# Encoder trunk on one core: sums leave GpSimd, convolution products stand ahead of their inverses, residual written in pieces

## Chip, cores and metric

One core of a Trainium2 chip runs the whole program. The metric is the device time of one execution in microseconds; lower is better. A core has five engines with a queue of instructions each: TensorE (PE, matmuls), VectorE (DVE), ScalarE (ACT), GpSimd (POOL) and SyncE (SP, which here only issues transfers). Each engine takes its own queue strictly in order and waits where an instruction needs what another engine has not yet made.

## The reference

Two layers over two inputs of batch 1 with shared weights, a prompt of 512 tokens and a sample of 256, of 1024 features, in float32. Each layer is a SwiGLU, a mixer (windowed attention on half of the features, a two-sided long convolution on the other half) and a second SwiGLU. Each is followed by a layer norm of the scaled residual plus the result.

```python
def _trunk(x, c, ...):
    for l in range(DEPTH):
        mod = (jax.nn.silu(c) @ ada_w[l] + ada_b[l]).reshape(B, N_MOD, D_MODEL)
        h = _modulate(x, mod[:, 0], mod[:, 1])
        f = _swiglu(h, ffn1_wi[l], ffn1_wo[l])
        x = _layer_norm(ALPHA * x + 0.5 * (1.0 + mod[:, 2][:, None, :]) * f, ln_g[l, 0], ln_b[l, 0])
        h = _modulate(x, mod[:, 3], mod[:, 4])
        z = h @ w_in[l]
        q, k, v, hz = jnp.split(z, [...], axis=-1)
...
        o_attn = _window_attention(q, k, v, sink[l])
        hz = _short_conv(hz, hy_conv_w[l], hy_conv_b[l])
        x0, x1, hv = jnp.split(hz, 3, axis=-1)
        filt = _hyena_filters(...)
        o_hy = _bidir_long_conv(hv * x1, filt, hy_bias[l]) * x0
        o = jnp.concatenate([_rms_norm(o_attn, grp_norm_g[l, :D_ATTN]),
                             _rms_norm(o_hy, grp_norm_g[l, D_ATTN:])], axis=-1) @ w_out[l]
        x = _layer_norm(ALPHA * x + (1.0 + mod[:, 5][:, None, :]) * o, ln_g[l, 1], ln_b[l, 1])
        h = _modulate(x, mod[:, 6], mod[:, 7])
        f = _swiglu(h, ffn2_wi[l], ffn2_wo[l])
        x = _layer_norm(ALPHA * x + 0.5 * (1.0 + mod[:, 8][:, None, :]) * f, ln_g[l, 2], ln_b[l, 2])
    return x
```

The long convolution (`_bidir_long_conv`) is a product of spectra: transform, multiply by the filter's spectrum, transform back.

## The kernel before

**Layout.** Features lie on the 128 partitions and the 768 tokens side by side, so `x`, `h` and the like are 8 tiles `d` of 128 x 768; `SEQ[0]` is the prompt's 512 columns and `SEQ[1]` the sample's 256. A float32 product is made from halves: ScalarE rounds a tile to its high half (`acopy`), another engine writes the low half `lo = x - hi` (a `tt`, a sum or difference of two tiles, on the engine named by `eng`), and TensorE makes three matmuls of the halves. Weights come as units of 128x1024 through SyncE's queue into a raw tile (`slot_r`), are split into a `slot_w` tile by `w_ahead`, and are taken in a fixed order by `w_take`. FFN products use a fast scheme of seven products; `joined` and `mixed` prepare its sums of activations and `prep_*` those of weights. Buffers are a few numbered slots per kind (`slot_s` 10 large ones, `slot_w` 6, `slot_r` 7, `slot_t` 6 scratch, `bank` 8 in PSUM); a new tile takes the slot that is free longest, and its writer waits for the last reader of the old one.

**Order.** There is no scheduler: the order on each engine is the order in which the Python code calls the operations. All instructions carry line L70, the wrapper that issues them, so the profile is read by tile names.

**The prologue.** `first_h` makes the first modulated input from `x`, then the loop at the end of `_program` runs six units of FFN 1 of layer 0 (`part[0].unit(i)`) with one `pump(1)` each. `pump` advances the ada steps, by which the modulation of later parts is computed: a step loads a 128x1024 block `ada_t` and takes two weighted sums of it on VectorE (CUSTOM_DVE) into `mods`. The very first also needs `silu(c)` on ScalarE from `c_row`. The residual's home in HBM, `x_spill`, is filled by one copy of `x_in` on GpSimd's queue.

**The mixer.** `run` in `mixer` orders it: units 4 to 11 are projections (4 to 9 with their short convolutions in `hyena_in`, 10 and 11 for `x0`), q/k/v groups follow with `side(i)` called after the i-th, then the attention's steps `u`. The convolution works on two halves `Hyena(0)` and `Hyena(1)` of the channels: `u_spectrum` transforms, `products(a)` multiplies the spectrum for frequency tiles `a` = 0, 1, 2 and splits the result, `inverse(a)` transforms it back on TensorE, `gate(i)` adds it to the output. A product with `a` below 2 is 16 multiplications, sums and low halves of 128x512, of which GpSimd makes 5 today (a third product term, and one low half); pm sums, the low halves of weights, of the RMS-normed groups (`Rms.apply`) and the sums of squares of attention blocks (`block_squares`) are GpSimd's too (`w_state["eng"] = gp` while the mixer runs).

**Norms and the residual.** `final` ends a part: output tiles come for the sample first, then for the prompt; `norm.add` sums `x` and its square over the tiles into `S` and `Q`, `norm.stats` and `bcast` make mean and scale, `norm.apply` writes the new `x` (a scale on GpSimd into `slot_s`) and the next `h`, `norm.low` its low halves. `after()` then writes the two halves `x.t[0]` and `x.t[1]` of the residual to `x_spill`, 1.5 MB each, and the next part's buffers take their slots.

## Time and profile before

| | us |
|---|---|
| median of 3 runs | 2977.01 (2975.27 to 2978.75) |
| the profiled execution | 2977.46 |
| its span on the core | 2975.2 |
| TensorE busy | 2853.4 |
| VectorE busy | 2101.6 |
| ScalarE busy | 1368.4 |
| GpSimd busy | 576.0 |
| mean granted TensorE clock | 0.982 of full speed |

The span is the time from the first to the last instruction; 2.3 us of the execution lie around it. Busy time of an engine is the sum of its instructions, so a stall of TensorE is the difference, and a stretch in which TensorE is granted half its clock counts as busy though it does half the work. What an idle engine waited for (its releaser) is inferred from semaphores. Times inside the span count from its start.

### The profile page before, as it was taken

Reading aid. Unit: us, or ns where it says so; the run is one execution under the profiler, and the core shown is the slowest. Engines: PE = TensorE matmul, PEld = TensorE weight load, DVE = VectorE, ACT = ScalarE, POOL = GpSimd, SP = SyncE. Lnnn points to the kernel's source line nnn. Section 1 sums busy time; section 2 is a strip of 40 time slices with the busy share of each in tenths; the row PEclk is TensorE's granted clock in tenths of the full one; section 3 lists DMA queues with packets and bytes.
Section 4 is the critical chain, followed back from the end, with each engine's and each line's share of the span. In section 5 each row is a group of like instructions: output and inputs, shape, how many; then the busy total and the mean of one; then the engine's idle time right before and its main releaser. Section 6 shows DMA issues by size and latency. Waiting matters only on the chain. (4 is left out here: it accounts for less than half of the span.)

```text
span 2975.2 us, 42222 instructions
## 1 busy us (share of the span) xinstructions
PE 2853.4 (96%) x16468; PEld 2608.0 (88%) x16468; DVE 2101.6 (71%) x3604; ACT 1368.4 (46%) x2355; POOL 576.0 (19%) x602
## 2 busy tenths in 40 slices
PE   9969999999899999999999999999989999999998
PEld 3769999998897889999988999999879788999997
DVE  5587888876858777778477878546686887444557
ACT  3534444444258454444444444444425854444444
POOL 2400000024532400000031000003453240000002
PEclk9989999999999999999999999999999999999999
DMA  5536655633111126654422665353311112454342
GB/s 199 199 120 177 181 162 153 176 142 121 50 46 69 64 109 182 191 180 135 112 101 112 191 186 149 106 120 121 114 57 65 58 43 114 85 114 107 99 109 84
DMA packets 99375, 364.65 MB, mean 123 GB/s; under 512 B 13542, under 2 KB 16823, under 8 KB 94648
## 3 DMA queue, kind: packets, MB, share of 16 engines
q1 hardware_dynamic: 74968, 259.88, 24.4%
q0 software_dynamic: 24208, 102.08, 15.8%
q8 instruction: 129, 2.11, 0.3%
q14 instruction: 70, 0.57, 0.1%
HBM read 284.33 MB, written 80.74 MB: 123 GB/s over the span
## 5 line engine op out<-in xcount | busy, mean ns | idle before, releaser
L70 PE MATMUL bank<-slot_s,slot_w 128*128 128x384 f32 (+2 forms) x13176 | 2331.9, 337 | 60.9 <-ACT slot_t L70 19.4
L70 PEld LDWEIGHTS bank<-slot_s,slot_w 128*128 128x128 f32 x13176 | 2140.2, 191 | 229.5 <-DVE slot_w L70 24.7
L70 POOL DMA_DIRECT2D x_spill<-slot_t x128 | 110.7, 865 | 1450.0 <-ACT slot_t L70 1442.8
L70 DVE CUSTOM_DVE_ANT_0 slot_t<-slot_r,slot_r 128x1024 bf16<-128x1024 f32 x256 | 311.9, 1223 | 104.9 <-DMA x_spill<-slot_t 44.2
L70 DVE TENSOR_TENSOR slot_w<-slot_w,slot_w 128x1024 fp32r<-128x1024 f32 (+2 forms) x444 | 370.2, 865 | 4.1 <-ACT slot_w L70 1.6
L70 ACT ACTIVATE slot_w<-slot_w 128x1024 fp32r<-128x1024 f32 (+1 forms) x298 | 249.7, 839 | 113.6 <-DVE slot_w L70 113.6
L70 ACT ACTIVATE slot_t<-bank,tiny 128x512 f32<-128x512 f32 (+1 forms) x256 | 147.4, 580 | 305.4 <-PE bank L70 302.0
L70 ACT ACTIVATE slot_w<-slot_r 128x1024 fp32r<-128x1024 f32 (+1 forms) x194 | 189.0, 992 | 175.2 <-DVE slot_r L70 114.5
L70 DVE TENSOR_TENSOR slot_w<-slot_r,slot_w 128x1024 fp32r<-128x1024 f32 (+1 forms) x148 | 172.7, 1178 | 113.3 <-ACT slot_w L70 113.1
L70 ACT ACTIVATE slot_t<-slot_t 128x384 f32<-128x384 f32 (+2 forms) x161 | 84.0, 526 | 333.1 <-DVE slot_t L70 333.0
L70 DVE TENSOR_TENSOR slot_t<-bank,slot_t 128x384 f32<-128x384 f32 x228 | 125.4, 555 | 145.7 <-PE bank L70 73.4
L70 ACT ACTIVATE slot_s<-slot_t 128x768 fp32r<-128x768 f32 (+2 forms) x160 | 113.0, 715 | 169.6 <-DVE slot_t L70 169.3
L70 ACT ACTIVATE slot_t<-bank 128x384 f32<-128x384 f32 (+3 forms) x282 | 139.6, 496 | 105.3 <-PE bank L70 102.8
L70 DVE TENSOR_TENSOR slot_s<-slot_t,slot_s 128x768 fp32r<-128x768 f32 (+2 forms) x170 | 144.8, 854 | 47.5 <-ACT slot_s L70 38.9
L70 PE MATMUL bank<-slot_s,slot_r 128*128 128x384 f32 x912 | 172.2, 337 | 0.0
L70 PEld LDWEIGHTS bank<-slot_s,slot_r 128*128 128x128 f32 x912 | 160.8, 188 | 0.0
L70 POOL TENSOR_TENSOR slot_w<-slot_r,slot_w 128x1024 fp32r<-128x1024 f32 (+1 forms) x46 | 100.1, 2178 | 157.5 <-ACT slot_w L70 139.0
L70 DVE TENSOR_TENSOR slot_r<-slot_w,slot_r 128x512 fp32r<-128x512 f32 x76 | 52.0, 685 | 107.2 <-ACT slot_r L70 107.2
L70 ACT ACTIVATE slot_t<-slot_s 128x256 f32<-128x256 f32 (+1 forms) x132 | 65.7, 509 | 108.7 <-DVE slot_s L70 100.2
L70 POOL TENSOR_TENSOR slot_t<-slot_t,slot_s 128x256 f32<-128x256 f32 (+1 forms) x91 | 95.1, 1045 | 60.6 <-DVE slot_s L70 55.6
L70 PE MATMUL bank<-slot_w,slot_s 128*128 128x256 f32 x864 | 106.4, 283 | 0.0
L70 PEld LDWEIGHTS bank<-slot_w,slot_s 128*128 128x128 f32 x864 | 104.2, 190 | 0.0
(138 smaller groups left out, 2331.1 us busy)
## 6 DMA issues: line engine op xcount, KB each, us to landing
slot_r<-w_units SPq DMA_DIRECT2D x170, 512.0 KB, 4.7
slot_w<-w_units SPq DMA_DIRECT2D x146, 512.0 KB, 4.1
slot_r<-ada_t SPq DMA_DIRECT2D x128, 512.0 KB, 6.0
x_spill<-slot_t POOLq DMA_DIRECT2D x128, 384.0 KB, 5.3
slot_s<-x_spill POOLq DMA_DIRECT2D x12, 1536.0 KB, 7.1
x_spill<-slot_s POOLq DMA_DIRECT2D x10, 1536.0 KB, 7.0
slot_r<-ada_nat SPq DMA_DIRECT2D x16, 512.0 KB, 5.4
g_main<-slot_s POOLq DMA_DIRECT2D x4, 1536.0 KB, 10.1
```

Source lines behind the costliest of these rows:

```text
L70: return getattr(real, name)(*args, **kwargs)
```

## The change

Seven things are done at once.

- Low halves of weights in the mixers, of the RMS-normed groups, the pm sums, the sums of attention squares and all parts of the spectral products go from GpSimd to VectorE. GpSimd's queue falls from 572 to 390 rows as printed.
- The norm's sample sums `S` and all its sums of squares `Q` go to VectorE; the prompt's `S` stays on GpSimd.
- `run` puts each product two units ahead of its inverse; of the second half, inverses 1 and 2 with their gates go into `side(0)` and `side(1)`.
- `final` calls `spill(s, j)`: the sample thirds of the residual go out before the prompt's apply, the first prompt half after tile 3, the second after tile 7.
- `x_spill` is filled by four copies in the loop over the units instead of one ahead of it.
- `first_h` writes the first four tiles straight to `fast.full`, which saves `joined(0)` to `joined(3)`; the other `joined` and `mixed` stand in units 0 and 1.
- The ada steps start in unit 2: one each in units 2 and 3, two each in 4 and 5.

```diff
-            tt(w[:, 1], raw, f32(w[:, 0]), ALU.subtract, eng=w_state["eng"])
+            tt(w[:, 1], raw, f32(w[:, 0]), ALU.subtract)
...
-                tt(self.S[:, c], self.S[:, c], x, ALU.add, eng=gp)
+                tt(self.S[:, c], self.S[:, c], x, ALU.add, eng=vec if s else gp)
                 self.sq = (d, s, sq)
 
         def squares(self):
             if self.sq is not None:
                 d, s, sq = self.sq
                 q = self.Q[:, SEQ[s]]
-                tt(q, q, sq, ALU.add, eng=vec if s or d % 2 else gp)
+                tt(q, q, sq, ALU.add)
...
+        for j in range(2):
+            spill(1, j)
         norm.low()
         norm.low()
         norm.squares()
@@ -577,9 +579,10 @@
                 norm.bcast(0)
                 for d in range(ND):
                     norm.apply(0, d)
+                    if d % 4 == 3:
+                        spill(0, d // 4)
                 norm.low()
                 norm.low()
-                after()
...
     def first_h(d):
         for c, s in ((SEQ[0], 0), (SEQ[1], 1)):
             affine(h[0](d, c), x(d, c), G[:, d, s:s + 1], B[:, d, s:s + 1])
-            v = slot_t([SLEN[s]])
+            v = slot_t([SLEN[s]]) if d > 3 else part[0].fast.full(d, c)
             if s:
                 affine(v, x(d, c), G[:, d, s:s + 1], B[:, d, s:s + 1])
             else:
                 ts(v, x(d, c), G[:, d, s:s + 1], B[:, d, s:s + 1])
             tt(h[1](d, c), v, f32(h[0](d, c)), ALU.subtract, eng=vec if s else gp)
 
+    part = swiglu(x, *h, 0, 0)
...
-    gp.dma_start(x_spill, x_in)
...
-                        tt(pm[c][:, bk, j, :], u[:, :, :P], u[:, :, :P - 1:-1], op, eng=gp)
+                        tt(pm[c][:, bk, j, :], u[:, :, :P], u[:, :, :P - 1:-1], op)
...
-                n = len(terms[0])
-                if n > 2:
-                    rest = term(1, 2, eng=gp)
-                    plus(rest, 1, 3, term(1, 3, eng=gp), eng=gp)
-                term(0, 0, Y[:, 0])
-                for i in range(1, n):
-                    plus(Y[:, 0], 0, i, term(0, i))
-                acopy(ys[:, 0, 0], Y[:, 0])
-                term(1, 0, Y[:, 1])
-                plus(Y[:, 1], 1, 1, term(1, 1))
-                tt(ys[:, 1, 0], Y[:, 0], f32(ys[:, 0, 0]), ALU.subtract, eng=gp)
-                if n > 2:
-                    tt(Y[:, 1], Y[:, 1], rest, ALU.add)
-                split_to(ys[:, 0, 1], ys[:, 1, 1], Y[:, 1])
+                for ri in range(2):
+                    y = Y[:, ri]
+                    for i, (gv, uv, minus) in enumerate(terms[ri]):
+                        p = slot_t([2, 256]) if i else y
+                        tt(p, gv, uv, ALU.mult)
+                        if i:
+                            tt(y, y, p, ALU.subtract if minus else ALU.add)
+                    acopy(ys[:, 0, ri], y)
+                    if ri:
+                        tt(ys[:, 1, 0], Y[:, 0], f32(ys[:, 0, 0]), ALU.subtract)
+                tt(ys[:, 1, 1], Y[:, 1], f32(ys[:, 0, 1]), ALU.subtract)
...
         def run(end):
-            w_state["eng"] = gp
             dfw = load_dft(dft_u, 1)
             proj.unit(4)
             proj.unit(5)
@@ -1387,27 +1378,25 @@
             hy0 = Hyena(0, u_spectrum(0, dfw))
             hy0.products(0)
             proj.unit(7)
-            hy0.inverse(0, dinv)
             hy0.products(1)
             proj.unit(8)
+            hy0.inverse(0, dinv)
             u_transposes(1)
-            hy0.inverse(1, dinv)
             hy0.products(2)
             proj.unit(9)
             hy0.gate(0)
+            hy0.inverse(1, dinv)
+            hy1 = Hyena(1, u_spectrum(1, dfw))
             hy0.gate(1)
             hy0.inverse(2, dinv)
-            hy1 = Hyena(1, u_spectrum(1, dfw))
-            hy0.gate(2)
             hy1.products(0)
             proj.unit(10)
-            hy1.inverse(0, dinv)
+            hy0.gate(2)
             hy1.products(1)
             proj.unit(11)
+            hy1.inverse(0, dinv)
+            hy1.products(2)
             hy1.gate(0)
-            hy1.inverse(1, dinv)
-            hy1.products(2)
-            hy1.gate(1)
 
             rms = [Rms(x0[0], 4, s) for s in range(2)]
             on_hy = []
@@ -1415,10 +1404,12 @@
 
             def side(i):
                 if i == 0:
-                    rms[0].squares()
+                    hy1.inverse(1, dinv)
+                    hy1.gate(1)
                 elif i == 1:
                     hy1.inverse(2, dinv)
                     hy1.gate(2)
+                    rms[0].squares()
...
-                tt(sq[:, 0:2], sq[:, 0:2], sq[:, 2:4], ALU.add, eng=gp)
-                tt(Q[0][:, cols], sq[:, 0], sq[:, 1], ALU.add, eng=gp)
+                tt(sq[:, 0:2], sq[:, 0:2], sq[:, 2:4], ALU.add)
+                tt(Q[0][:, cols], sq[:, 0], sq[:, 1], ALU.add)
...
-                    rms_at[1].apply(on_at, (0, 1), eng=gp)
+                    rms_at[1].apply(on_at, (0, 1))
...
-        def spill():
-            for j in range(2):
-                gp.dma_start(x_spill[:, 4 * j:4 * j + 4, :], x.t[j])
+        def spill(s, j):
+            gp.dma_start(x_spill[:, 4 * j:4 * j + 4, SEQ[s]], x.t[j][:, :, SEQ[s]])
...
-    part = make_part(0, x, h)
     for i in range(2 * NHEAD):
         part[0].unit(i)
-        pump(1)
-        if i == 0:
-            part[0].fast.load(NHEAD)
-        elif i < 5:
-            part[0].fast.joined(i - 1)
-            part[0].fast.joined(i + 3)
-            part[0].fast.mixed(i - 1)
+        if i < 2:
+            part[0].fast.load(NHEAD) if i == 0 else None
+            for d in (2 * i, 2 * i + 1):
+                part[0].fast.joined(d + 4)
+                part[0].fast.mixed(d)
+        else:
+            pump(2 if i > 3 else 1)
+            gp.dma_start(x_spill[:, 2 * i - 4:2 * i - 2, :], x_in[:, 2 * i - 4:2 * i - 2, :])
```

**TensorE at the second inverse of the first half, layer 0.** `slot_w..._w3` holds the inverse transform and the other `slot_w` of those rows the product; the rows with `slot_s` are a projection unit, those with `ident` the transposes. Before:

```order
L70 MATMUL bank3_874_6383<-ident_65,slot_t0_856_6246 128x128 [waits Pool_49]
L70 MATMUL bank3_874_6383<-ident_65,slot_t1_823_6012 128x128
L70 MATMUL bank3_874_6383<-ident_65,slot_t0_856_6246 128x128 [waits Pool_49]
L70 MATMUL bank7_875_6390<-slot_w3_828_6043,slot_w5_859_6281 128x256 [waits Activation_49]
L70 MATMUL bank7_875_6390<-slot_w3_828_6043,slot_w5_859_6281 128x256
L70 MATMUL bank7_875_6390<-slot_w3_828_6043,slot_w5_859_6281 128x256 [waits Pool_49]
L70 MATMUL bank7_875_6390<-slot_w3_828_6043,slot_w5_859_6281 128x256 x3
L70 MATMUL bank7_875_6390<-slot_w3_828_6043,slot_w5_859_6281 128x256 [waits Activation_49]
L70 MATMUL bank7_875_6390<-slot_w3_828_6043,slot_w5_859_6281 128x256
L70 MATMUL bank7_875_6390<-slot_w3_828_6043,slot_w5_859_6281 128x256 [waits DVE_49]
L70 MATMUL bank7_875_6390<-slot_w3_828_6043,slot_w5_859_6281 128x256 x15
L70 MATMUL bank2_880_6429<-slot_s5_756_5376,slot_w4_853_6236 128x512
```

After, in the same queue:

```order
L70 MATMUL bank2_872_6398<-slot_s6_762_5454,slot_w4_845_6229 128x256 x2
L70 MATMUL bank2_872_6398<-slot_s8_763_5457,slot_w4_845_6229 128x256
L70 MATMUL bank2_872_6398<-slot_s6_762_5454,slot_w4_845_6229 128x256
L70 MATMUL bank0_875_6459<-slot_w3_820_6036,slot_w5_850_6249 128x256 [waits DVE_49,Activation_49]
L70 MATMUL bank0_875_6459<-slot_w3_820_6036,slot_w5_850_6249 128x256 x23
L70 MATMUL bank1_877_6485<-slot_s2_863_6361,slot_w0_804_5881 128x256 [waits DVE_49,Activation_49]
L70 MATMUL bank1_877_6485<-slot_s2_863_6361,slot_w0_804_5881 128x256 [waits DVE_49]
L70 MATMUL bank1_877_6485<-slot_s2_863_6361,slot_w0_804_5881 128x256 x4
L70 MATMUL bank5_878_6493<-slot_s2_863_6361,slot_w0_804_5881 128x256 [waits PE_49]
```

Before, the inverse stands right behind the transposes and waits four times, for ScalarE, GpSimd, ScalarE and VectorE, as the halves of its product arrive. After, a whole unit stands between, the inverse has one wait ahead of it, and the spectrum of the second half (`dft`) follows.

**VectorE behind the third weight split, prologue.** ISA rows are the two sums of an ada step (`mods`), `slot_w` a weight split, `slot_r5`, `slot_s` and `slot_t` the FFN's activations. Before:

```order
L70 TENSOR_TENSOR slot_w5_206_967<-slot_r6_178_781,slot_w5_206_967 128x1024 [waits DMAHW2_49,Activation_49]
L70 ISA slot_t5_211_981,mods0_79<-slot_r2_209_975,slot_r0_202_911 128x1024 [waits DMAHW7_49,Activation_49,Pool_49]
L70 ISA mods0_79 128x1
L70 ISA slot_t5_211_981,mods0_79<-slot_r2_209_975,slot_r1_203_912 128x1024 [waits DVE_49,Activation_49]
L70 ISA mods0_79 128x1
L70 TENSOR_TENSOR slot_w0_216_1039<-slot_r4_199_889,slot_w0_216_1039 128x1024 [waits DMASW0_49,DMAHW3_49,PE_49,Activation_49]
L70 TENSOR_TENSOR slot_t2_208_972<-slot_t2_208_972,bank5_214_989 128x512 [waits PE_49,Pool_49]
L70 TENSOR_TENSOR slot_s8_218_1044<-slot_t2_208_972,slot_s8_218_1044 128x512 [waits DMASW0_49,Activation_49]
L70 TENSOR_TENSOR slot_t2_208_972<-slot_t2_208_972,bank2_215_990 128x256 [waits PE_49]
L70 TENSOR_TENSOR slot_s8_218_1044<-slot_t2_208_972,slot_s8_218_1044 128x256 [waits Activation_49]
L70 ISA slot_t0_219_1051,mods0_79<-slot_r3_210_977,slot_r0_202_911 128x1024 [waits DMAHW0_49,Pool_49]
```

After:

```order
L70 TENSOR_TENSOR slot_w5_199_959<-slot_r6_171_774,slot_w5_199_959 128x1024 [waits DMAHW2_49,Activation_49]
L70 TENSOR_TENSOR slot_r2_203_970<-slot_s7_162_735,slot_s8_164_739 128x768 [waits DMAHW3_49,PE_49,Pool_49]
L70 TENSOR_TENSOR slot_t2_207_975<-slot_r2_203_970,slot_s4_151_652 128x384 [waits DVE_49,Pool_49]
L70 SCALAR_TENSOR_TENSOR slot_t2_207_975<-slot_t2_207_975,slot_s4_151_652 128x384 [waits DVE_49]
L70 SCALAR_TENSOR_TENSOR slot_r2_203_970<-slot_t2_207_975,slot_r2_203_970 128x384 [waits DVE_49]
L70 TENSOR_TENSOR slot_s4_151_652<-slot_s4_151_652 128x384
L70 TENSOR_TENSOR slot_s0_204_972<-slot_t2_207_975,slot_s0_204_972 128x768 [waits Activation_49]
L70 TENSOR_TENSOR slot_s6_206_974<-slot_r2_203_970,slot_s6_206_974 128x384 [waits Activation_49]
```

Before, the ada step stands ahead of the split of the fourth unit's weight (`slot_w0` here) and the flush of a unit's result. After, the activation sums of `joined` and `mixed` stand there, and the first ada step follows 34 rows later than before.

**GpSimd at the end of the norm after FFN 1, layer 0.** TENSOR_SCALAR rows are the scales that write the new residual. Before:

```order
L70 TENSOR_SCALAR slot_s1_714_5030<-slot_t2_796_5686,lnp_72 128x512 [waits DVE_49]
L70 TENSOR_SCALAR slot_s1_714_5030<-slot_t5_797_5693,lnp_72 128x512 [waits DVE_49]
L70 TENSOR_SCALAR slot_s1_714_5030<-slot_t3_798_5700,lnp_72 128x512 [waits DVE_49]
L70 TENSOR_SCALAR slot_s1_714_5030<-slot_t0_799_5707,lnp_72 128x512 [waits DVE_49,Activation_49]
L70 DMA x_spill_915<-slot_s4_713_5028 128x3072 [waits Pool_49]
L70 DMA x_spill_915<-slot_s1_714_5030 128x3072 [waits Pool_49]
L70 TENSOR_TENSOR slot_t4_805_5852<-slot_t1_804_5844 128x128 [waits DVE_49,Activation_49]
```

After:

```order
L70 DMA x_spill_908<-slot_s2_705_5019 128x4x256
L70 DMA x_spill_908<-slot_s1_706_5021 128x4x256
L70 TENSOR_TENSOR tiny2_779_5582<-tiny2_779_5582,mhalf_81 128x4 [waits DVE_49]
L70 TENSOR_TENSOR tiny2_779_5582<-tiny2_779_5582 128x4 [waits Pool_49]
L70 TENSOR_SCALAR slot_s2_705_5019<-slot_t2_784_5653,lnp_72 128x512 [waits DVE_49,Activation_49]
L70 TENSOR_SCALAR slot_s2_705_5019<-slot_t1_785_5659,lnp_72 128x512 [waits DVE_49,Activation_49]
L70 TENSOR_SCALAR slot_s2_705_5019<-slot_t4_786_5665,lnp_72 128x512 [waits DVE_49,Activation_49]
L70 TENSOR_SCALAR slot_s2_705_5019<-slot_t5_787_5672,lnp_72 128x512 [waits DVE_49,Activation_49]
L70 DMA x_spill_908<-slot_s2_705_5019 128x4x512 [waits Pool_49]
L70 TENSOR_SCALAR slot_s1_706_5021<-slot_t3_788_5680,lnp_72 128x512 [waits DVE_49,Activation_49]
```

Before, both 128x3072 transfers come behind the last scale. After, the two sample thirds go out ahead of the prompt's scales, the first prompt half in the middle of them, and one 128x4x512 piece stays for the end.

## Rows read from the trace of the kernel before

**Rows 1.** The page: busy time, share of the span, instructions.

```profile
PE 2853.4 (96%) x16468; PEld 2608.0 (88%) x16468; DVE 2101.6 (71%) x3604; ACT 1368.4 (46%) x2355; POOL 576.0 (19%) x602
```

**Rows 2.** TensorE's waits by releaser: total us, times, longest.

```profile
PE bank L70 <- DVE slot_w L70: 27.8, 32, 6.5
PE bank L70 <- ACT slot_w L70: 26.9, 16, 10.4
...
PE bank L70 <- DVE slot_s L70: 13.7, 14, 2.4
```

**Rows 3.** Windows: busy us of PE, PEld, DVE, ACT, POOL, then granted clock.

```profile
152.00:212.00 60.00, 37.31 (x177) 31.61 (x178) 51.90 (x81) 16.47 (x27) 0.00 (x0) 0.82 0.32 113
744.00:800.00 56.00, 50.21 (x307) 44.89 (x306) 46.33 (x58) 18.21 (x30) 29.20 (x19) 0.94 0.18 66
800.00:845.00 45.00, 40.71 (x291) 38.10 (x290) 36.69 (x62) 16.41 (x32) 18.13 (x11) 0.96 0.11 36
860.00:980.00 120.00, 110.18 (x717) 97.13 (x716) 88.65 (x279) 89.04 (x222) 36.53 (x36) 0.97 0.20 71
774.20:781.00 6.80, 5.70 (x24) 4.98 (x23) 5.08 (x10) 4.16 (x7) 2.39 (x1) 0.50 0.21 77
1088.20:1095.10 6.90, 5.65 (x18) 5.66 (x19) 5.71 (x10) 4.19 (x8) 0.00 (x0) 0.51 0.00 0
```

**Rows 4.** Timelines of the prologue (start, us, instruction, idle before) and a transfer.

```profile
127.00 25.73 PE L70 MATMUL bank<-slot_s,slot_w 128*128 128x512 f32 x144 [2.94 <-DVE slot_w L70]
...
159.21 10.03 PE L70 MATMUL bank<-slot_s,slot_w 128*128 128x512 f32 x46 [6.48 <-DVE slot_w L70]
...
198.71 1.01 PE L70 MATMUL bank<-slot_s,slot_w 128*128 128x384 f32 x2 [10.40 <-ACT slot_w L70]
...
218.68 6.50 PE L70 MATMUL bank<-slot_s,slot_w 128*128 128x384 f32 x34 [0.25 <-DVE slot_w L70]
...
155.40 1.23 DVE L70 CUSTOM_DVE_ANT_0 slot_t<-slot_r,slot_r 128x1024 bf16<-128x1024 f32 x1 [26.19 <-DMA slot_r<-ada_t]
...
165.57 0.95 DVE L70 TENSOR_TENSOR slot_r<-slot_s,slot_s 128x768 f32<-128x768 f32 x1
...
170.03 1.22 DVE L70 TENSOR_TENSOR slot_w<-slot_r,slot_w 128x1024 fp32r<-128x1024 f32 x1
...
x_spill<-x_in POOLq DMA_DIRECT2D x1, 24.1
```

**Rows 5.** Timelines of the mixer's convolution, and VectorE's splits from 1120 to 1540.

```profile
772.37 0.50 PE L70 MATMUL bank<-slot_w,slot_w 128*128 128x256 f32 x2 [2.58 <-ACT slot_w L70]
...
825.90 11.57 PE L70 MATMUL bank<-slot_w,slot_s 128*128 128x256 f32 x96
...
745.42 0.69 DVE L70 TENSOR_TENSOR slot_t<-slot_s,slot_s 128x512 f32<-128x512 f32 x1
...
746.76 1.79 DVE L70 TENSOR_TENSOR slot_t<-slot_s,slot_s 128x512 f32<-128x512 f32 x1
...
L70 DVE TENSOR_TENSOR slot_w<-slot_r,slot_w 128x1024 fp32r<-128x1024 f32 x24 | 29.2, 1222 | 12.3 <-ACT slot_w L70 12.2
```

**Rows 6.** Timelines of the attention part.

```profile
897.71 2.37 POOL L70 TENSOR_TENSOR slot_w<-slot_r,slot_w 128x1024 fp32r<-128x1024 f32 x1 [6.37 <-issue]
...
897.78 2.32 DVE L70 TENSOR_TENSOR tiny<-tiny 128x4 f32<-128x4 f32 x1
...
901.59 0.30 PE L70 MATMUL bank<-ident,slot_w 128*128 128x128 f32 x1 [2.28 <-DVE slot_w L70]
...
920.41 1.31 POOL L70 TENSOR_TENSOR slot_t<-slot_t 128x256 f32<-128x256 f32 x2 [11.33 <-ACT slot_t L70]
```

**Rows 7.** Chain of waits and timelines where the residual is written, layer 1.

```profile
2461.62 8.54 DMA x_spill<-slot_s
...
2470.26 0.53 ACT L70 ACTIVATE slot_s<-slot_r 128x384 fp32r<-128x384 f32 x1 [3.78 <-DMA x_spill<-slot_s]
...
2495.75 4.53 PE L70 MATMUL bank<-slot_s,slot_w 128*128 128x384 f32 x13 [4.37 <-ACT slot_t L70]
```

More of the change, by code (lines that the diff above doesn't have):

```diff
@@ L233, in _program @@
     w_raw, w_split = {}, {}
-    w_state = {"dma": 0, "split": 0, "next": 0, "eng": vec, "limit": w_stops.pop(0), "raws": 3}
+    w_state = {"dma": 0, "split": 0, "next": 0, "limit": w_stops.pop(0), "raws": 3}
     def w_load(upto):
@@ L545, in sample_out, with final @@
         drain()
-    def final(os, norm, proj, n_head, after=None):
+    def final(os, norm, proj, n_head, spill):
         sample_out(os, norm)
@@ L1358, in bcast, with apply @@
                 self.R = spread(self.st[:, 4:8], NTOK[self.s])
-            def apply(self, on, cs=range(4), eng=vec):
+            def apply(self, on, cs=range(4)):
                 c_, n = SEQ[self.s], SLEN[self.s]
@@ L1365, in low @@
                     hi, lo, v = late.pop(0)
-                    tt(lo, v, f32(hi), ALU.subtract, eng=eng)
+                    tt(lo, v, f32(hi), ALU.subtract)
                 for c in cs:
@@ L1432, in side @@
                 elif i == 5:
-                    rms[0].apply(on_hy, (0,), eng=gp)
-                    rms[1].apply(on_hy, (0, 1), eng=gp)
+                    rms[0].apply(on_hy, (0,))
+                    rms[1].apply(on_hy, (0, 1))
                 elif i == 6:
@@ L1437, in side @@
                     att[0].scores(0)
-                    rms[0].apply(on_hy, (1,), eng=gp)
+                    rms[0].apply(on_hy, (1,))
                 elif i == 7:
@@ L1675, in attention @@
                 if u == 1:
-                    rms[0].apply(on_hy, (2, 3), eng=gp)
+                    rms[0].apply(on_hy, (2, 3))
                 elif u == 2:
-                    rms[1].apply(on_hy, (2, 3), eng=gp)
+                    rms[1].apply(on_hy, (2, 3))
                     reload()
@@ L1686, in attention @@
                 elif u == 8:
-                    rms_at[1].apply(on_at, (0, 1), eng=gp)
+                    rms_at[1].apply(on_at, (0, 1))
                 elif u == 11:
                     on_at.append(slot_s([2, 2, T], F32R))
-                    rms_at[1].apply(on_at, (2, 3), eng=gp)
+                    rms_at[1].apply(on_at, (2, 3))
                 adds = [filler() for _ in range(share[u - 1])]
@@ L1725, in attention @@
             o_at.hooks.update({2: hook1, 3: hook2})
-            w_state["eng"] = vec
             return end([o_at], xn, coef)
```

7 lines of the change are left out of this document (removed).

## The prediction

> **What bounds the kernel now.** The page comes first: TensorE is busy for 96% of the span [rows 1], so nearly all that can be won is time in which TensorE stands or runs at its lower clock. The profiled execution took 2977.46 us, 2.3 us more than its span and 0.45 us more than the median of 2977.01, so a sum made on the trace can be read against the median as it stands. Next come TensorE's waits: some 28 us each behind weight tiles of VectorE and ScalarE, 14 us behind activations of VectorE [rows 2]. The reader is to see that the releaser is almost always an engine that writes the low half of a split, or a copy in front of one. Third are the windows: the waits stand in bunches, in the prologue, in the two mixers and at three places where the residual is written out, and behind each bunch TensorE runs for 3.4 to 14 us at a granted clock of 0.50, which is its 1.2 GHz level, after it had stood for some us [rows 3]. A wait so costs its own time and half of what TensorE does in the stretch behind it. The clock gate here is known only from such rows.
>
> **Prologue.** The first six units of layer 0 are separated by one ada step each: two 1.23 us sums on VectorE that must wait for an ada block. At 155.40 VectorE had stood for 26.19 us for that block, behind a copy of the input that took 24.1 us from issue to landing [rows 4]. The weight split behind it came late, and TensorE stood 6.48 us; then VectorE was busy almost without a gap to 206 with four pairs of joined and mixed (165.57 to 170.03, 4.46 us a pair), ada steps and splits, and TensorE stood 10.40 us [rows 4]. In 152 to 212 TensorE was busy 37.31 of 60 us, so it stood 22.7, and some 9 us of its work was done at the lower clock, which lost about 4 [rows 3]: 27 us in all. After the change the pairs come first (4 x 4.46 = 18 us, from about 129 to 148, in time in which VectorE now stands), and the six ada steps follow later, two at a time only in the last two units. Six units of 25.73 / 3 = 8.58 us from 127.0 [rows 4] end at 178.5, and VectorE's queue then decides. Its blocks have landed at about 160; four steps of 2.4, one split, one flush and the sums of the first fast set (about 6) end at 180, some 2 us behind TensorE's first need of them. Another flush (3), two steps (5), activation sums (3) and the low half of the next set (4) end at 195, and TensorE, with 60 matmuls at 0.17 us in front, is there at 191. So it resumes there at 195, where it now resumes at 218.68 [rows 4]. **Gain 23.** The ends: 12, if the weights of the fourth unit still come late behind the same copy, and 27, without any wait. The input copy in four pieces is issued at the same place of GpSimd's queue in effect, since nothing before it there waits for the units; I cost it at nothing.
>
> **Products two units ahead of their inverses.** Today an inverse starts at once behind its product: at 772.37 it waited 2.58 us for ScalarE's half, and then for the halves of VectorE and GpSimd [rows 5]. The windows 744 to 845 hold 10.1 us of standing (56.0 - 50.21 and 45.0 - 40.71) and the stretches at the lower clock lose some 4.5 more (6.8 us at 774, of which 5.70 busy [rows 3], and a stretch half as long later), 14.6 us a layer. These waits go. What is late next is VectorE, which takes over the third of the product that was GpSimd's, the pm sums and the splits. From 744.8 on, by the rows for VectorE alone (0.69 us for a 128x512 sum, of which the next one overlaps .08; 1.22 for a split [rows 5]): four products of 10.8 us, one of 5.3, five splits of 1.15, a conv pair of 4.5 and three of 2.45, transposes 1.9 and gates 1.8. That is 69.8 us, and ends with the second weight of the first q/k/v group at about 814. TensorE begins that group at 825.90 [rows 5]; without the standing before it (9.6), the loss at the lower clock (4.5) and one inverse that now comes later (24 matmuls, 3.1) it wants the weight at 808.7. So a new wait of 5 us appears there, and a dip behind it of 1.5. **Gain 8 a layer, 16 for both.** The ends are 3 (VectorE another 5 us late) and 11 (the wait overlaps with a dip that comes anyway).
>
> **Sums leave GpSimd in the attention part.** Both operands in SBUF is the case that matters. On VectorE one 128x512 sum took 0.69 us with GpSimd idle and 1.79 beside a GpSimd sum [rows 5]; a 128x4 sum took 2.32 us at 897.78, until the GpSimd split of 897.71 ended, and TensorE stood 2.28 us for the weights behind it [rows 6]. The Trainium skill, page "SBUF — State Buffer", section "Who interferes with whom", has this as one exclusive lock, held for the whole instruction; the rows agree, and by it alone the change would repay all that VectorE loses beside GpSimd. Against that stand the instructions VectorE takes over from 860 to 980: 7 splits x 1.22 (2.39 on GpSimd [rows 6]), 12 low halves of 0.43 or 0.69, 12 sums of squares of 0.2 or 0.43, in all 18.4 us on top of 88.65 busy in 120 [rows 3]. What GpSimd's overlap costs VectorE there I put at 6 us (seven splits at about 0.9 us of blocking), so VectorE gains some 12 us of work. And it now waits, in its order, for ScalarE's squares: GpSimd at 920.41 had stood 11.33 us for them [rows 6], which cost no one anything. The twelve steps here hand over from TensorE to VectorE to ScalarE and back, and ScalarE is as busy as VectorE (89 of 120 us [rows 3]), so I take two thirds of the added work as on the path. **Loss 8 a layer, 16 for both**, between 0 (all of it lies in VectorE's gaps) and 12.
>
> **The residual written in pieces.** Today two transfers of 1.5 MB are issued at the end of the norm; the second lands 8.54 us after its issue, ScalarE waits 3.78 us for the tile it frees, VectorE behind it, and TensorE stands 4.37 us at 2491, some 25 us later [rows 7]. The same gap of 4.4 stands at 1085 and 1613, and behind two of the three the clock falls for 6.9 us (5.65 busy at 1088 [rows 3]), behind one for half as long: 13.1 + 2 x 2.8 + 1.4 = 20 us. After the change the sample thirds go out long before, the first prompt piece some 8 us before the last, and 1 MB is left. If 3 MB take 8.5 us, 1 MB and the rest of its forerunner take 4 to 5, so the tile is free at 2466.5, where ScalarE asks for it. **Gain 16**, ends 4 and 20. The two to three issues of 0.6 us that stand among GpSimd's scales there are hidden while GpSimd waits for VectorE's part of each scale; uncovered they would cost 2 us. A rule speaks against this part. The Trainium skill, page "SBUF — State Buffer", section "SBUF: two separate sides", says that descriptors of a transfer issued from GpSimd can't be written while VectorE holds the port pair in one of its fast modes. No row here shows a transfer held up in that way, and it is a rival below.
>
> **The rest.** Around the norms that lead into the mixer and into the second FFN, sample sums of 128x256 go to VectorE; the waits behind VectorE's activations, 13.7 us in all [rows 2], stand mostly there. Half of that goes, with a little of the clock: **gain 8**, the end of the program among it, between 0 and 14.
>
> **Sum.** 23 + 16 - 16 + 16 + 8 = 47 us; 2977.5 - 47 = 2930.5, so 2930.
>
> **Rivals.**
> 1. *The attention part loses nothing.* VectorE's durations beside GpSimd fall to their values alone, and its gaps (31 us of 120 [rows 3]) take the rest. For it: one blocked sum there cost TensorE 2.28 us [rows 6]. Against it: the waits for ScalarE are in VectorE's order now. 2930 - 16, with small gains, 2912.
> 2. *The prologue keeps half its stall*, since the weights and ada blocks come at the rate of a backlog of some 12 MB and not by the order: 2941 to 2950.
> 3. *The pieces land no earlier*: more and smaller runs on one queue, and VectorE busier while they are prepared. 16 - 4 fewer: 2942. By the rule cited above it would be this one.
> 4. *VectorE becomes what TensorE waits for throughout the mixers*, the one that ends on the other side. Per layer VectorE takes over about 41 us (17 splits, 12 product sums, 6 lows, 4 pm sums, and the 18 of the attention part, at the lengths above). If it is late at the first q/k/v group already and never catches up, all of this reaches TensorE, and only the 10 us of standing in the convolution goes: +31 a layer, 2977.5 + 62 - 47 = 2992. It decides from 24 us lost in each mixer, since the other parts bring 23 + 16 + 8. Against it: VectorE has some 18 + 31 us of gaps a layer in these windows [rows 3]. A half of it, with the conv part winning nothing and the attention part losing 12, gives 2954.
> 5. *The change doesn't do what it says*: the four input pieces stand no later in effect. That is so and is costed; the remaining edits can't fail to move.
>
> **How the numbers follow.** My forecast (2918 to 2941) has 0.50, rival 1 0.17, rivals 2 and 3 0.12 and 0.09, the half of rival 4 0.07, rival 4 in full 0.04, and 0.01 remains for the unforeseen. The range reaches from 2908, somewhat under rival 1, to 2956, just over the half of rival 4, and leaves out about 2 in 10, mixtures at both ends included. About 0.2%, 6 us, is what a measurement of this kernel can tell from no change. Only rival 4 reaches that border or beyond: faster 0.94, same 0.02, slower 0.04.
>
> **What would show it.** Prologue: TensorE's 6.48 and 10.40 us waits gone, the third product's start some 24 us earlier; if the first unit's weights split still waits behind an ada block, I was wrong. Convolution: no wait at any inverse of the first half, VectorE's 128x512 sums all near 0.69, and one wait of about 5 us behind VectorE at the first q/k/v group. Attention: VectorE near 100 of 120 us, TensorE's standing up from 10 to 18 us. Pieces: no ScalarE wait for a spill, and the 4.4 us gaps under 1. The prediction fails if VectorE's idle time in the mixers vanishes, or if a piece issued from GpSimd lands later than 5 us.

## The result and the profile after

| | before | after |
|---|---|---|
| median | 2976.14 us (4 runs, 2973.57 to 2978.75) | 2938.78 us (4 runs, 2933.28 to 2941.24) |
| profiled execution, its span | 2977.46, 2975.2 | 2938.19, 2936.2 |
| mean granted TensorE clock | 0.982 | 0.987 |

The ratio of the medians is 0.9872 (95% interval 0.9855 to 0.9889): 37.4 us or 1.3% less, well clear of the spread of the runs. The kernel is faster, 9 us above the predicted 2930, inside the range.

The page's line on busy time, of after (answers [rows 1]):

```profile
PE 2837.5 (97%) x16468; PEld 2594.4 (88%) x16468; DVE 2139.2 (73%) x3821; ACT 1367.5 (47%) x2355; POOL 331.8 (11%) x394
```

TensorE does the same 16468 matmuls in 16 us less busy time, since less of them runs at its lower clock (mean granted clock 0.987 for 0.982). GpSimd has given away 244 us of work, and VectorE's busy time grew by 38 only. TensorE's waits of after by releaser (total us, times, longest; answers [rows 2]):

```profile
PE bank L70 <- DVE slot_w L70: 30.0, 26, 3.2
PE bank L70 <- DVE slot_s L70: 27.6, 18, 4.3
PE bank L70 <- ACT slot_t L70: 11.4, 10, 2.4
...
PE bank L70 <- ACT slot_w L70: 1.9, 3, 0.8
```

Of the 26.9 us behind ScalarE's weights 1.9 are left, those behind VectorE's weights are not (27.8 before), and those behind VectorE's activations have doubled (13.7 before). The places differ now, so the totals don't tell which part of the change did what. Both kernels issue the same matmuls in nearly the same order, so the same matmul can be found in both traces by its number; its time in one less its time in the other is what has been gained up to there. Between the borders of the parts this gives:

| stretch | predicted gain | gain, layer 0 / 1 |
|---|---|---|
| prologue | 23 | 24.5 |
| FFN 1 to the mixer's norm | in "the rest" | 2.4 / 1.7 |
| convolution | 8 a layer | 9.4 / 9.2 |
| attention | -8 a layer | -10 / -10 |
| norm from mixer to FFN 2 | in "the rest" | -2.2 / -1.5 |
| residual, three places | 16 | 5.9, 4.6, 4.8 |

With 0.3 elsewhere these sum to 39.1 us, against 39.3 between the profiled executions.

**Prologue.** TensorE's timeline of after, and VectorE's first ada step (start, us, instruction, idle before and its releaser; answers [rows 4]):

```profile
125.14 54.04 PE L70 MATMUL bank<-slot_s,slot_w 128*128 128x512 f32 x310 [1.38 <-DVE slot_w L70]
181.58 3.30 PE L70 MATMUL bank<-slot_s,slot_w 128*128 128x384 f32 x13 [2.40 <-ACT slot_t L70]
185.89 6.56 PE L70 MATMUL bank<-slot_s,slot_w 128*128 128x384 f32 x25 [1.01 <-DVE slot_s L70]
192.70 6.50 PE L70 MATMUL bank<-slot_s,slot_w 128*128 128x384 f32 x34 [0.25 <-DVE slot_w L70]
```
```profile
156.15 1.23 DVE L70 CUSTOM_DVE_ANT_0 slot_t<-slot_r,slot_r 128x1024 bf16<-128x1024 f32 x1 [1.24 <-DMA slot_r<-ada_t]
```

VectorE's first ada step starts at 156.15, as late as before, but VectorE now stands 1.24 us for its block instead of 26.19, having made the activation sums meanwhile. Six units run without a stop for 54 us, and the group of 34 matmuls that began at 218.68 now begins at 192.70.

**Convolution.** TensorE and VectorE of after in layer 0 (as above; answers [rows 5]):

```profile
759.43 2.53 PE L70 MATMUL bank<-slot_s,slot_w 128*128 128x256 f32 x12 [4.34 <-DVE slot_s L70]
...
787.23 0.38 PE L70 MATMUL bank<-slot_w,slot_s 128*128 128x256 f32 x1 [0.76 <-ACT slot_w L70]
788.49 4.46 PE L70 MATMUL bank<-slot_w,slot_s 128*128 128x256 f32 x35 [0.88 <-DVE slot_w L70]
...
751.02 0.68 DVE L70 TENSOR_TENSOR slot_r<-slot_r,slot_s 128x512 f32<-128x512 f32 x1
...
757.75 2.44 DVE L70 SCALAR_TENSOR_TENSOR slot_s<-bank,convp,slot_s 128x511 f32<-128x511 f32 x4
```

In the last two rows VectorE makes `products(2)` from 751.02 on, then a weight split, and only then unit 9's short convolution at 757.75, which frees the banks that the spectrum of the second half wants. TensorE waits 4.34 us for it. At the q/k/v group 1.64 us are left.

**Attention.** The stretch 824 to 954 of after holds the matmuls of 860 to 980 before, begun 36 us earlier and 10 us longer (busy us of PE, PEld, DVE, ACT, POOL, granted clock; answers [rows 3]); then TensorE's longer waits there (answers [rows 6]):

```profile
824.00:954.00 130.00, 113.46 (x721) 98.56 (x721) 92.64 (x308) 89.50 (x222) 3.50 (x5) 0.96 0.19 65
```
```profile
866.46 1.94 PE L70 MATMUL bank<-ident,slot_w 128*128 128x128 f32 x8 [3.05 <-DVE slot_w L70]
...
900.98 1.00 PE L70 MATMUL bank<-ident,slot_w 128*128 128x128 f32 x4 [2.17 <-DVE slot_w L70]
...
941.40 2.02 PE L70 MATMUL bank<-ident,slot_w 128*128 128x128 f32 x8 [3.20 <-DVE slot_w L70]
```

TensorE stands 16.5 us, where it stood 9.8, and is busy 3.3 us longer, though VectorE is busy for 92.64 us, only 4 more than before.

**Residual.** Transfers (count, KB, median us from issue to landing), the last piece in layer 0, and TensorE at the same matmul, first in before, then in after (answers [rows 7]):

```profile
x_spill<-slot_s POOLq DMA_DIRECT2D x10, 1024.0 KB, 4.6
```
```profile
1031.28 0.79 POOL L70 DMA_DIRECT2D x_spill<-slot_s  x1 [0.39 <-POOL slot_s L70]
```
```profile
1089.45 15.36 PE L70 MATMUL bank<-slot_s,slot_w 128*128 128x384 f32 x72 [4.36 <-ACT slot_t L70]
```
```profile
1062.23 13.20 PE L70 MATMUL bank<-slot_s,slot_w 128*128 128x384 f32 x72 [1.71 <-ACT slot_t L70]
```

The last 1 MB lands 4.6 us after its issue, and no engine waits for a piece any more.

### The profile page after: what moved, and what is told of

Same layout as the page of the kernel before. It is cut to its first block, busy times and chain, and to the rows that moved or that the text cites. A ratio compares the mean times of both kernels' runs of the same rounds, so it can differ in the third digit from the quotient of the medians.

```text
span 2936.2 us, 42164 instructions
## 1 busy us (share of the span) xinstructions
PE 2837.5 (97%) x16468; PEld 2594.4 (88%) x16468; DVE 2139.2 (73%) x3821; ACT 1367.5 (47%) x2355; POOL 331.8 (11%) x394
## 3 DMA queue, kind: packets, MB, share of 16 engines
q1 hardware_dynamic: 74968, 259.88, 24.5%
## 5 line engine op out<-in xcount | busy, mean ns | idle before, releaser
L70 DVE TENSOR_TENSOR slot_w<-slot_r,slot_w 128x1024 fp32r<-128x1024 f32 (+1 forms) x194 | 222.0, 1153 | 113.4 <-ACT slot_w L70 111.9
L70 DVE TENSOR_TENSOR slot_s<-slot_t,slot_s 128x768 fp32r<-128x768 f32 (+2 forms) x190 | 153.1, 810 | 52.6 <-ACT slot_s L70 48.4
L70 DVE SCALAR_TENSOR_TENSOR slot_t<-bank,slot_t 128x384 f32<-128x384 f32 x76 | 42.3, 556 | 83.4 <-PE bank L70 82.2
L70 DVE SCALAR_TENSOR_TENSOR slot_s<-bank,tiny,slot_s 128x256 f32<-128x256 f32 (+1 forms) x160 | 87.0, 564 | 15.1 <-PE bank L70 14.9
```

The source lines that it names most:

```text
L70: return getattr(real, name)(*args, **kwargs)
```

## The experiments

Where one run is given, it stands beside one run of the kernel before (2975.59, 2975.24 or 2972.12 us). Four runs of after lie between 2933 and 2941, so a difference of some 8 us between single runs proves little. The stretches below, from the alignment of matmuls, tell more: a run that leaves a part as it is in after has that part's stretch within some 2 us of after's.

**The prologue alone**, put into the kernel before:

```diff
-    gp.dma_start(x_spill, x_in)
...
-            v = slot_t([SLEN[s]])
+            v = slot_t([SLEN[s]]) if d > 3 else part[0].fast.full(d, c)
...
-        pump(1)
...
+        if i < 2:
...
+                part[0].fast.joined(d + 4)
+                part[0].fast.mixed(d)
+        else:
+            pump(2 if i > 3 else 1)
+            gp.dma_start(x_spill[:, 2 * i - 4:2 * i - 2, :], x_in[:, 2 * i - 4:2 * i - 2, :])
```

> The kernel before with the prologue's part of the change alone (activation sums in units 0 and 1, ada steps from unit 2 on, input copied in four pieces, first_h writing straight to fast.full). My theory, that the order on VectorE set the two stalls of 6.5 and 10.4 us: TensorE's matmul number 900 comes 23 to 26 us earlier than before, everything behind it is shifted by the same amount, and the span falls to about 2951. The rival, that the backlog of transfers sets it and other parts of the change helped: at most 12 us, span 2963 or more.

2950.73 us, 24.9 less than before. All of it is there after the prologue and is kept to the end: this part works by itself, and nothing behind it takes the gain back. The order of the ada steps and the four saved sums of `first_h` are not taken apart here.

**One copy of the input**, the rest of after kept:

```diff
+    gp.dma_start(x_spill, x_in)
...
-            gp.dma_start(x_spill[:, 2 * i - 4:2 * i - 2, :], x_in[:, 2 * i - 4:2 * i - 2, :])
```

> The changed kernel with the input copied to its home in HBM by one transfer ahead of the units, as before, in place of four pieces. My theory, that the pieces stand at the same place in effect and the order on VectorE does it: within 2 us of the changed kernel at matmul 900, span about 2936 to 2938. The rival, that the pieces take the copy off the weights' way: 8 to 12 us later, span about 2945 to 2948.

2943.16 us, between the two forecasts of the span. In the prologue the group of 192.70 starts at 193.89, 1.2 us later, but at the 900th matmul this run is 0.5 us ahead of after. So the stall went through the order on VectorE, not through the copy in pieces. Some 4.5 us lie behind three later writes of the residual, with short stretches at the lower clock, which this edit doesn't touch; why they came in this run is open.

**The residual written whole**, at the end of the norm as before:

```diff
-                    if d % 4 == 3:
-                        spill(0, d // 4)
...
+                spill()
```

> The changed kernel with the residual written in two whole halves at the end of the norm, as before. My theory, that the last 1.5 MB half holds up ScalarE's next tile: the gaps of about 4.4 us behind the three norms come back with their stretches at 1.2 GHz, 4.5 to 6 us at each place, 15 us in all, span about 2951. The rival, that VectorE's sums and not the transfers moved these gaps: under 5 us in all, span under 2941.

2951.17 us, 12.4 above after's median. The alignment has 4.6, 4.8 and 5.2 us at the three places, together 14.6, and the old rows are back:

```profile
1039.04 0.53 ACT L70 ACTIVATE slot_s<-slot_r 128x384 fp32r<-128x384 f32 x1 [3.82 <-DMA x_spill<-slot_s]
...
1064.52 14.38 PE L70 MATMUL bank<-slot_s,slot_w 128*128 128x384 f32 x72 [4.34 <-ACT slot_t L70]
```

This part is settled: a tile freed later holds up ScalarE, and some 25 us later TensorE.

**The old order of products and inverses**, with all sums on VectorE:

```diff
             proj.unit(7)
+            hy0.inverse(0, dinv)
             hy0.products(1)
             proj.unit(8)
-            hy0.inverse(0, dinv)
             u_transposes(1)
+            hy0.inverse(1, dinv)
             hy0.products(2)
...
-                    hy1.inverse(1, dinv)
-                    hy1.gate(1)
+                    rms[0].squares()
```

> The changed kernel with the order of products, inverses and gates as before (each inverse right behind its product), all sums still on VectorE. My theory, that the distance between product and inverse brings the 9 us a layer: the waits in front of the inverses come back, longer than before since VectorE makes the whole product (about 1 to 4 us at each of five), and the span rises by 15 to 30 us to 2951 to 2966. The rival, that leaving GpSimd brings it: under 4 us a layer, span under 2944.

2941.35 us. My theory fell: in the convolution the order brings 1.1 us in layer 0 and 2.1 in layer 1. TensorE's waits in layer 0 are these:

```profile
741.92 4.47 PE L70 MATMUL bank<-slot_w,slot_w 128*128 128x256 f32 x22 [3.52 <-DVE slot_w L70]
...
784.07 4.24 PE L70 MATMUL bank<-slot_w,slot_w 128*128 128x256 f32 x22 [2.33 <-DVE slot_w L70]
```

They sum to 5.85 us, against 4.34 + 1.64 = 5.98 in after. An inverse that starts straight behind its product waits, but the product that stands ahead makes the next engine step wait about as long.

**The convolution's sums back on GpSimd**, in the new order:

```diff
-                        tt(pm[c][:, bk, j, :], u[:, :, :P], u[:, :, :P - 1:-1], op)
+                        tt(pm[c][:, bk, j, :], u[:, :, :P], u[:, :, :P - 1:-1], op, eng=gp)
...
+                if n > 2:
+                    rest = term(1, 2, eng=gp)
+                    plus(rest, 1, 3, term(1, 3, eng=gp), eng=gp)
...
+                tt(ys[:, 1, 0], Y[:, 0], f32(ys[:, 0, 0]), ALU.subtract, eng=gp)
...
+            w_state["eng"] = gp
```

> The changed kernel, new order of products and inverses kept, with the mixer's sums back on GpSimd up to the attention part (low halves of weights, pm sums, the third term and one low half of each product). With the old order on VectorE alone the time was only 2.6 us above the changed kernel's, so my revised theory is that leaving GpSimd brings most of the convolution's gain: here 5 to 9 us a layer are lost again, by 128x512 sums of 1.1 to 1.8 us on VectorE, span 2946 to 2954. My first theory, that the distance between product and inverse brings it: within 2 us a layer, span 2936 to 2940.

2956.69 us, 17.9 above after's median; some 10 us in each layer by the alignment, so the whole gain of the convolution. VectorE's sums of one form by shape (count, busy us, mean ns), from 740 to 845 in the kernel before, from 700 to 845 in this kernel, and from 700 to 845 in after:

```profile
L70 DVE TENSOR_TENSOR slot_r<-slot_r,slot_t 128x512 f32<-128x512 f32 x24 | 26.4, 1101 | 1.0
```
```profile
L70 DVE TENSOR_TENSOR slot_r<-slot_r,slot_t 128x512 f32<-128x512 f32 x24 | 26.4, 1101 | 1.0
```
```profile
L70 DVE TENSOR_TENSOR slot_r<-slot_r,slot_t 128x512 f32<-128x512 f32 x28 | 19.4, 692 | 1.0
```

What one such sum waits for is seen in this kernel's timeline:

```profile
754.74 0.68 DVE L70 TENSOR_TENSOR slot_t<-slot_r,slot_s 128x512 f32<-128x512 f32 x1
...
755.04 1.50 POOL L70 TENSOR_TENSOR slot_w<-slot_r,slot_w 128x512 fp32r<-128x512 f32 x1 [5.26 <-ACT slot_w L70]
...
755.46 1.64 DVE L70 TENSOR_TENSOR slot_r<-slot_r,slot_t 128x512 f32<-128x512 f32 x1
...
761.09 2.90 PE L70 MATMUL bank<-slot_s,slot_w 128*128 128x256 f32 x12 [5.37 <-DVE slot_s L70]
```

GpSimd's split ends at 756.54, and VectorE's sum 0.56 us after that, though its record begins at 755.46. TensorE then stands 5.37 us where it stood 4.34 in after. The run with the old order, this one, before and after make two by two. Against before, the new order without the move gains -0.8 and -0.4 us in the two layers, the move off GpSimd without the new order 8.3 and 7.1, both together 9.4 and 9.2. So the engine brings nearly all of it. Whether by VectorE's shorter sums alone is not shown: GpSimd's own sums are also gone from TensorE's path, and in this kernel TensorE stands 2.0 of 14 us from 700 to 850 for a weight of GpSimd. The Trainium skill, page "SBUF — State Buffer", section "SBUF: two separate sides", says that a VectorE instruction with two SBUF inputs and a GpSimd instruction that reads SBUF exclude each other for a whole instruction; these rows agree (0.69 us alone, 1.64 behind a 1.50 us split).

**Attention squares back on GpSimd**:

```diff
-                tt(sq[:, 0:2], sq[:, 0:2], sq[:, 2:4], ALU.add)
-                tt(Q[0][:, cols], sq[:, 0], sq[:, 1], ALU.add)
+                tt(sq[:, 0:2], sq[:, 0:2], sq[:, 2:4], ALU.add, eng=gp)
+                tt(Q[0][:, cols], sq[:, 0], sq[:, 1], ALU.add, eng=gp)
```

> The changed kernel with the attention's sums of squares back on GpSimd (12 small sums a layer). If VectorE's wait in order for ScalarE's squares (1.5 to 2.1 us of standing before each) is a part of the attention's 10 us: the gaps of TensorE at 884 and 938 shrink, 2 to 4 us a layer are won, span 2928 to 2932. If the mere load of VectorE is the cause, or GpSimd's blocking takes it back: within 1 us a layer, span 2934 to 2938.

2931.97 us; 3.9 and 4.2 us a layer in the attention part, the size that I had expected if VectorE's wait for ScalarE's squares is a part of the loss. The edit also takes the sums themselves off VectorE, so it doesn't tell the wait from the load.

**Low halves of weights back on GpSimd, in the attention steps only**:

```diff
+            w_state["eng"] = gp
...
+            w_state["eng"] = vec
```

> The changed kernel with the low halves of the weights split during the attention steps back on GpSimd (four or so a layer, 2.4 us each there). If VectorE's wait for ScalarE's copy (1.0 to 1.8 us) and the 1.2 us of the split ahead of the softmax's scaling cause the gaps of 3.0, 2.2 and 1.2 us: these go. But a GpSimd sum of 2.4 us blocks VectorE's small sums behind it, as at 897.78 in the kernel before. I expect the two to cancel: within 3 us a layer either way, span 2932 to 2942. The rival, that the blocking costs nothing: 5 us or more a layer are won, span under 2927.

2930.53 us; 3.1 and 3.4 us a layer won, where I had expected the blocking to eat the gain.

**Both**: the two edits above together.

> The changed kernel with both the sums of squares and the low halves of weights of the attention steps back on GpSimd. Each alone brought 3 to 4 us a layer. If they relieve different steps: 5 to 7 us a layer, span 2921 to 2926. If what is left is bound by the handing over between VectorE and ScalarE, or GpSimd's blocking grows: no more than one of them alone, span 2928 to 2933.

2922.28 us; 5.7 and 6.8 us a layer. So some 6 of the 10 us that the change loses here came with these two groups of sums. Unlike in the convolution, moving them to VectorE did not pay. Each is a sum that waits for ScalarE, and on GpSimd that wait held up nobody: this reason is argued, and the next run tests a part of it.

**Softmax scaling ahead of splits and squares; `products(2)` behind unit 9**:

```diff
-            hy0.products(2)
...
+            hy0.products(2)
...
-                if done:
-                    block_squares(done.pop())
+                if u < 12:
+                    at.norms(u)
```

> The changed kernel with two moves in the order and none between engines: in each attention step the softmax's scaling stands ahead of the weight splits, the normed groups' low halves and the sums of squares; and in the convolution the third product stands behind unit 9. If waiting in order is what costs (VectorE standing for ScalarE ahead of work that TensorE needs), the gaps of 3.0, 2.2, 1.2 and 3.2 us in the attention steps and the one of 4.3 us at the second half's spectrum fall: 8 to 14 us a layer, span 2908 to 2920. If VectorE's load is what costs, the gaps move elsewhere: under 3 us a layer, span above 2930.

2930.39 us, at the rival's border: 3.5 and 4.9 us a layer won in the attention part, 1.1 and 0.6 lost in the convolution, where the wait moved to an inverse:

```profile
758.86 4.60 PE L70 MATMUL bank<-slot_w,slot_w 128*128 128x256 f32 x24 [4.06 <-ACT slot_s L70]
...
868.49 2.45 PE L70 MATMUL bank<-slot_r,slot_t 128*128 128x512 f32 x5 [1.71 <-DVE slot_r L70]
```

The 3.05 us wait of 866.46 is gone, but 1.71 stands behind another tile of VectorE (`slot_r`) a few us later. No work changes its engine here, so the place of the sums in VectorE's queue explains a third to a half of the loss of 10; it is not the whole of it.

**Every second prompt `Q` sum back on GpSimd**:

```diff
-                tt(q, q, sq, ALU.add)
+                tt(q, q, sq, ALU.add, eng=vec if s or d % 2 else gp)
```

> The changed kernel with the prompt's sums of squares of every second tile back on GpSimd, as before. At the end of the mixer VectorE is busy without a gap from 985 to 1005, and TensorE stands 5.2 us and runs 10.2 us at 1.2 GHz there, against 4.2 and 6.8 before. If the moved sums are the cause: 2 to 3 us a layer come back at that place, span 2929 to 2933. If GpSimd's sums, by blocking VectorE, are the cause: no change or worse, span 2935 to 2940.

2933.47 us; at the norm from mixer to FFN 2 0.6 us in layer 0 and 0.8 in layer 1, not the 2 to 3 expected. Inconclusive.

**The prompt's `S` sums on VectorE too**:

```diff
-                tt(self.S[:, c], self.S[:, c], x, ALU.add, eng=vec if s else gp)
+                tt(self.S[:, c], self.S[:, c], x, ALU.add)
```

> The changed kernel with the norms' prompt sums on VectorE too, so that GpSimd keeps only the scales there. VectorE takes 7 sums of 0.69 us more per norm (4.8 us) and loses the blocking by GpSimd's sums (low halves of 1.19 instead of 0.41 us, 1.8 instead of 0.69). If blocking is what costs at the end of the mixer: 2 us or more a layer are won, span under 2933. If load is what costs: 2 to 4 us a layer are lost there, span 2939 to 2946.

2932.82 us; 2.4 and 1.8 us won at the norms into the mixer, though in layer 0 runs that change nothing there win up to 2; 1.0 and 0.3 won at the norm into FFN 2. Neither moving sums to VectorE nor back settles that norm.

**A version that takes what won**: both groups of attention sums on GpSimd, the prompt's `S` on VectorE, softmax scaling first.

> The changed kernel with what the runs so far favoured: the attention steps' sums of squares and low halves of weights back on GpSimd, the prompt's norm sums on VectorE, and the softmax's scaling ahead of the normed groups' low halves. By the single runs: 13 to 16 us for the first, 1 to 3 for the second; for the third, the two gaps left in front of it (2.7 and 3.0 us a layer) shrink if waiting in order makes them, 2 to 4 us a layer: 2914 to 2920. If these gaps are bound by VectorE's load and only move, 2920 to 2924. Either way clearly faster than both kernels.

2919.45 us, median of 5 runs (2915.18 to 2921.72), against 2974.76 of 8 runs of before: ratio 0.9813 (0.9799 to 0.9827). It beats both kernels, the changed one by 0.66%. The time lies at the border of the two forecasts. By the alignment the attention part wins 6.7 and 7.2 us a layer, so with both groups on GpSimd the softmax's place adds 1.0 and 0.4, not the 2 to 4 expected. Waits and attention window:

```profile
PE bank L70 <- DVE slot_s L70: 24.8, 18, 4.3
...
PE bank L70 <- DVE slot_w L70: 12.3, 18, 1.4
```
```profile
860.00:980.00 120.00, 109.27 (x626) 93.28 (x627) 96.97 (x269) 78.00 (x189) 18.71 (x22) 0.99 0.17 58
```

## Why the prediction was right, and where not

**Prologue: right, 24.5 for 23.** The 6.48 and 10.40 us waits are gone, and the product resumed at 192.70 where I had 195. In between TensorE waited 2.40 us for ScalarE and 1.01 and 0.25 for VectorE, where I had VectorE alone. That the copy in pieces costs nothing was right; it also brings nothing there that lasts.

**Convolution: the sum was nearly right, by luck; the reason was not.** I had 14.6 us of waits and lost clock taken away by the distance between product and inverse, and a new wait of 5 us plus a dip left over. The gain was 9.4 and 9.2, and a wait of 4.34 us did come. But the step "these waits go", because an inverse no longer starts behind its product, failed: with the old order and the sums on VectorE 8.3 and 7.1 us of the gain are there all the same. What removed the waits was that the sums left GpSimd; VectorE's fell from 1.10 to 0.69 us each, which I take to be the way, though GpSimd's own slower sums went with it. The second miss is the place: I followed VectorE's queue only to the first q/k/v group, and put its lateness there. It came earlier, at the first thing behind a product that TensorE needs, a bank freed by unit 9's convolution.

**Attention: right in sign and nearly in size, wrong in one term.** The loss was 10 a layer for 8. I had VectorE at about 100 of 120 us, 18.4 added and 6 repaid by the missing overlap. For the same matmuls it was at 92.64 of 130, 4 us more than before, so against the 18.4 some 14 were repaid and not 6, and the standing of TensorE still rose to 16.5 for my 18. The mis-sized step is the 6 us, and two thirds of the added work "on the path" was the wrong way to count the rest: by that rule 4 us of added work lose under 3. That 8 came near 10 is the luck of two errors that offset each other. Moving two groups of sums back won 5.7 and 6.8 us, and moving only their places in the queue 3.5 and 4.9. Rival 1, that nothing is lost here, had its first condition met, since VectorE's small sums fell to about half, and was still wrong. The row of the blocked 128x4 sums over the whole span (count, busy us, mean ns | idle), of before and of after:

```profile
L70 DVE TENSOR_TENSOR tiny<-tiny 128x4 f32<-128x4 f32 x29 | 9.0, 311 | 15.2 <-ACT tiny L70 14.9
```
```profile
L70 DVE TENSOR_TENSOR tiny<-tiny 128x4 f32<-128x4 f32 x29 | 4.6, 157 | 2.1 <-ACT tiny L70 2.0
```

**Residual: right, 15.3 for 16,** by the expected mechanism, shown by the run that writes it whole. The last 1 MB landed at 4.6 us for my 4 to 5; TensorE's wait there fell to 1.71 us, not under 1. Rival 3 is out for the piece that counts. Some earlier pieces landed later than the 5 us that I had named as a sign of failing, a sample third 6.1 us after its issue at 1004.53 and a first prompt piece 6.7 us after 2067.33; no engine waited for them, and why they were late is open.

**The rest: the failing term of the sum.** I had +8 for the norms and the end. It was 4.1 at the norms into the mixer and -3.7 at the norms into FFN 2, and 0.3 elsewhere, 0.7 in all. I took half of TensorE's waits behind VectorE's activations as won without a reason from the rows; they grew from 13.7 to 27.6 us in all, and at that norm VectorE had no time to spare, before or after. The windows there of before, then of after with the stretch at the lower clock, and two of TensorE's waits in after (columns as above):

```profile
1012.00:1034.00 22.00, 17.73 (x84) 14.92 (x83) 21.59 (x40) 13.16 (x23) 16.29 (x16) 0.84 0.15 49
```
```profile
984.00:1010.00 26.00, 20.82 (x98) 17.79 (x97) 24.37 (x45) 13.54 (x24) 16.94 (x17) 0.80 0.24 79
...
998.90:1009.10 10.20, 7.04 (x29) 6.46 (x30) 10.10 (x19) 4.59 (x8) 5.37 (x6) 0.50 0.38 116
```
```profile
1000.06 2.00 PE L70 MATMUL bank<-slot_s,slot_w 128*128 128x256 f32 x6 [2.39 <-DVE slot_s L70]
...
1004.07 1.44 PE L70 MATMUL bank<-slot_s,slot_w 128*128 128x256 f32 x5 [2.00 <-DVE slot_s L70]
```

VectorE was busy for 21.59 of 22 us before, a row that I hadn't asked for. TensorE ran at 0.50 of its clock, the 1.2 GHz level, for 10.2 us there, where it had been 6.8 before. That VectorE's load is the cause was argued from these rows; the two runs that moved sums there (`Q` back, `S` over) both won 1 us or less there and don't show it.

In sum: 47, less 7.3 for this term, 4 for the attention part and 0.7 for the residual, plus 1.5 for the prologue and 2.6 for the convolution, is 39.1.

## What to carry to other kernels

Before a sum is moved from GpSimd, ask both what it blocks there and what it waits for: on VectorE its wait holds up all that stands behind it. The kind of sum alone does not decide. In the attention part two groups that wait for ScalarE were better left on GpSimd, but in the convolution the split of 755.04 had itself waited 5.26 us for ScalarE and then blocked VectorE; the sums there were only moved together, and together they were better on VectorE. When an engine takes over work, follow its queue to the first thing behind that work that TensorE needs, not only to the end of the stretch, and look at its busy time in each window that gets an addition: a stretch in which it is busy without a gap wins nothing. A large product moved away from its consumer takes its place ahead of another consumer; test the order apart from the engine.

## What the runs showed of the hardware

With GpSimd busy for 47.33 of 101 us [rows 3], VectorE's 128x512 sums of one form with two SBUF operands took 1.10 us on average, and 0.69 without it: 60% more over the whole convolution. Yet GpSimd is not dear everywhere: in the last kernel it is busy for 18.71 of the 120 us shown above, and TensorE stands 10.7 us in that window. In the changed kernel, the same window holds 3.88 us of GpSimd, and TensorE stands 15.6:

```profile
860.00:980.00 120.00, 104.42 (x599) 88.50 (x598) 91.42 (x271) 77.75 (x193) 3.88 (x4) 0.96 0.13 44
```

(The last kernel is 5 to 12 us ahead in its work there, by the alignment.)
